# Splitting weights ahead at a fixed pace in the MLPs alone, with four chunk buffers there, and bias broadcasts issued two at a time from ScalarE's queue

## The chip, the cores and the metric

The kernel runs on one core of one Trainium2 chip. The metric is the device time of one execution in microseconds (us), taken as the median of several executions. Five engines work side by side, each through its own instructions in its own order: TensorE (PE in the rows; its weight loads are PEld), VectorE (DVE), ScalarE (ACT), GpSimd (POOL) and SyncE (SP). SP, ACT and POOL also issue the transfers (DMA), which sixteen DMA engines of the core carry.

## What is computed

The reference runs two transformer blocks, one after the other, over 512 tokens of width 1024. The first has two layers: a short-convolution mixer, an MLP, a sparse-attention mixer (NSA) and another MLP. The second block (a state-space branch and windowed attention, merged, then a gated feed-forward) follows, and the change doesn't touch it.

```
for layer in range(2):
    h = rms_norm(x, norm_mix[layer])
    if layer == 0:  x = x + short_conv_mixer(h, a_w_in, a_conv_w, a_w_out)
    else:           x = x + nsa_mixer(h, b_w_qg, b_w_o, shared, rel_bias)
    x = x + squared_relu_mlp(rms_norm(x, norm_mlp[layer]), mlp_w1[layer], mlp_w2[layer])
    if layer == 0:  shared = nsa_shared_kv(rms_norm(x, kv_norm), w_kv, ...)
squared_relu_mlp(h, w1, w2) = square(relu(h @ w1)) @ w2
```

All of it is in float32. The attention adds a bias per head and distance, which comes from a small table (`rel_bias`).

## The kernel before

**Products.** Each product of two float32 matrices is made from three TensorE matmuls on a rounded type (fp32r): both operands are split into a high part (the value rounded) and a low part (what the rounding left), and high by high, high by low and low by high are added up in PSUM. For activations the parts are called `hh`/`hl`, `a`/`b` or `yh`/`yl`, for weights `whi`/`wlo`. A matmul here takes a 128x128 weight block against 512 token columns.

**The weight stream.** All weights lie in device memory as 362 chunks of 128x1024 (512 KB), in the order in which they are used; a chunk holds eight weight blocks, and four blocks are a half. `Stream.pre` loads a chunk into one of two buffers (`w32`, on SP's queue), and splits halves up to three ahead of the one in use: ScalarE makes `whi` (L200, L207), VectorE makes `wlo` (L209), each in four buffers. `take` hands out the next block, and calls `pre` at each half. Layer A (the mixer) uses chunks 0 to 31, the first MLP (MLP0) 32 to 95, NSA 96 to 132, the second MLP (MLP1) 133 to 196.

**Splits ahead.** `Stream.ahead` (called once a chunk by `take`) makes the low parts of 112 later chunks, those of NSA and of the second block's mixer (`NSA_CH`, `MIX_CH`), beforehand: GpSimd's queue loads the chunk (`aw`, L161), ScalarE makes its high part (`ah`, L168 or L172), VectorE its low part (`al`, L169 or L173), and GpSimd's queue writes that back to device memory (`dlo`, L174). Later `pre` loads it instead of computing it. The tiles `aw` and `al` have two buffers, `ah` one. Some chunks are also scaled by a vector on the way, in four pieces (L168, L169) instead of one. Splits ahead are made in layer A, from the time when ten chunks have been asked for, in MLP0 and in MLP1, three for every four chunks.

**Biases.** In layer A, after the second output block (`f == 1`), `biases` multiplies the table with one-hot rows (six small matmuls) into `line` in device memory, and spreads each of its 16 rows over 128 rows of the arrays `sk1`, `sk2` and `sk3`, each row one element further: 48 transfers from device memory to device memory, 16 each of 320, 192 and 72 KB, issued on GpSimd's queue (L622). Attention later reads skewed rows from them.

**The order of the work.** The program is recorded as written, and a scheduler that simulates it then sets the order of the instructions on each engine. The order is fixed when the program is built, and each engine carries out its own in that order, waiting on semaphores. So a split ahead stands where that simulation put it, which may be far ahead of the place where `ahead` was called, and an engine that waits at one holds up all that stands behind it. A transfer signals on one of eight semaphores of its kind (`DMAHW0` to `DMAHW7` for SP and ACT, `DMASW0` to `DMASW7` for POOL), taken in turn; a later transfer on the same one waits until the earlier has landed.

Of the kernel before, what the change touches and what calls it, by code (L numbers as in the profile page):

```python
# [47 lines left out]
MIX_CH = (197, 272)  # L48
AHEAD0 = 10

# [75 lines left out]
class Stream:  # L126
    def __init__(self, b, pool, src, nch):
# [11 lines left out]
        self.owed = 0  # L139

    def scaled(self, half):
        g, ks = self.plan[half]
        n = 512 // len(ks)
        for i, k in enumerate(ks):
            yield slice(i * n, i * n + n), self.b.pv(g, k)

    def ahead(self):
        if self.ap is None or not self.todo or self.nd < AHEAD0:
            return
        self.owed += 3  # L150
        if self.owed < 4:
            return
        self.owed -= 4
        nc = self.b.nc
        c = self.todo.pop(0)
# [6 lines left out]
        if 2 * c in self.plan or 2 * c + 1 in self.plan:  # L162
            for o in range(2):
                e = slice(o * 512, o * 512 + 512)
                ws, hs, ls = w[:, e], h[:, e], l[:, e]
                parts = self.scaled(2 * c + o) if 2 * c + o in self.plan else [(slice(0, 512), 1.0)]
                for a, sc in parts:
                    nc.scalar.activation(out=hs[:, a], in_=ws[:, a], func=AF.Copy, scale=sc)  # L168
                    nc.vector.scalar_tensor_tensor(out=ls[:, a], in0=ws[:, a], scalar=sc, in1=hs[:, a].bitcast(F32),  # L169
                                                   op0=ALU.mult, op1=ALU.subtract)  # L170
        else:
            nc.scalar.activation(out=h, in_=w, func=AF.Copy)  # L172
            nc.vector.tensor_tensor(out=l, in0=w, in1=h.bitcast(F32), op=ALU.subtract)  # L173
# [10 lines left out]
    def pre(self, half):  # L184
        b, nc = self.b, self.b.nc
        while self.nd < min(self.nch, half // 2 + 2):
            t = self.pool.tile([P, 1024], F32, tag="w32", name="w32", bufs=2)
            nc.sync.dma_start(t, self.src[self.nd])
            self.w32[self.nd] = t
            self.nd += 1  # L190
# [41 lines left out]
class Builder:  # L232
# [230 lines left out]
    def first(self):  # L463
# [15 lines left out]
        with ExitStack() as c:  # L479
            ps = c.enter_context(tc.tile_pool(name="psA", bufs=1, space=PSUM))  # L480
            self.ps1 = lambda: ps.tile([P, 512], F32, tag="mm", bufs=7, name="mm")
            self.pst = lambda: ps.tile([P, 512], F32, tag="st", bufs=1, name="st")
            self.st.ap = c.enter_context(tc.tile_pool(name="ahead", bufs=1))
            with ExitStack() as c2:
                self.yp = c2.enter_context(tc.tile_pool(name="la", bufs=1))
                self.layer_a()
            if self.stop == "a":
                return
            self.mlp("mlp_w1_0", "mlp_w2_0", "g_mlp0")
            self.st.ap = None  # L490
# [16 lines left out]
    def layer_a(self):  # L507
# [14 lines left out]
        for f in range(KD):  # L522
            pcs = []
            for part in (1, 2, 0):
                if f == 0 and part:
                    p = (p1, p2)[part - 1]
                else:
                    p = self.ps1()
                    self.gemm([(p, XS)], "a_w_in", 0, part * 1024 + f * 128, hs)
                pcs.append(p)  # L530
                if f == 0 and part == 0:
# [25 lines left out]
        for m in range(KD):  # L557
            p = self.ps1()
            self.gemm([(p, slice(0, 512))], "a_w_out", 0, m * 128, ys)
            x = self.xs[m]  # L560
            nc.vector.tensor_tensor(out=x[:, XS], in0=p, in1=x[:, XS], op=ALU.add)
# [38 lines left out]
    def biases(self):  # L600
# [18 lines left out]
        self.sk3 = self.dr.tile([16, 128 * 145], F32, name="sk3")  # L619
        for h in range(16):  # L620
            for sk, a, n in ((self.sk1, 0, 640), (self.sk2, OH_A, 384), (self.sk3, OH_A + 384, 144)):
                nc.gpsimd.dma_start(sk[h:h + 1, :].rearrange("o (q w) -> (o q) w", w=n + 1)[:, 0:n],  # L622
                                    self.line[h:h + 1, a:a + n].to_broadcast([128, n]))

# [1256 lines left out]
```

## Time and profile before

| | us |
|---|---|
| Median of 3 runs | 2486.36 |
| Lowest and highest of them | 2483.63, 2491.55 |
| Profiled execution: its own time | 2476.05 |
| Profiled execution: span, first to last instruction | 2474.3 |
| Busy in that span: PE, PEld, DVE, ACT, POOL | 97%, 84%, 66%, 50%, 19% |

The profiled execution is one more run, 10 us below the median of the others, and 1.75 us of its time lie outside the span. Matmuls overlap, so a busy share near 100% doesn't say that TensorE goes at its best pace: how many matmuls it starts in a stretch says that.

### The profile page before, as it was taken

How to read it: one execution, taken by the hardware profiler on the slowest of the kernel's cores; microseconds unless marked ns; L12 is line 12 of the kernel's file. 1: busy time of each engine (PE TensorE's matmuls, PEld its weight loads, DVE VectorE, ACT ScalarE, POOL GpSimd, SP SyncE). 2: the span in 40 equal slices, each digit the busy share in tenths (PEclk: the TensorE clock that was granted, in tenths of full speed). 3: DMA queues.
4: the chain of work that ended last, by engine and by line, in shares of the span. 5: the costliest groups of instructions: out<-in, count | busy, mean ns of one | idle time of the engine just before them, and what ended most of it. 6: DMA issues, size and time to landing. Idle time of an engine off the chain costs nothing.

```text
span 2474.3 us, 38734 instructions
## 1 busy us (share of the span) xinstructions
PE 2391.7 (97%) x14273; PEld 2078.8 (84%) x14273; DVE 1624.5 (66%) x3293; ACT 1231.0 (50%) x2431; POOL 471.5 (19%) x657
## 2 busy tenths in 40 slices
PE   7999999999899999999999999999999999999997
PEld 5777777887787777777888999999999999998996
DVE  8657855543777768746636895569776566864873
ACT  6436543333677765434344776556555334432442
POOL 2333221001333322221022222122322100000001
PEclk9999999999999999999999999999999999999998
DMA  7898886335743347887335354543335452333322
GB/s 277 271 266 289 303 306 223 95 117 166 242 129 93 120 144 255 297 283 278 103 94 195 114 149 148 166 152 121 125 125 162 141 196 86 95 94 94 92 88 77
DMA packets 151739, 418.93 MB, mean 169 GB/s; under 512 B 22603, under 2 KB 29003, under 8 KB 151499
## 3 DMA queue, kind: packets, MB, share of 16 engines
q1 hardware_dynamic: 115024, 287.70, 36.3%
q0 software_dynamic: 35392, 127.49, 15.4%
q8 instruction: 112, 1.84, 0.3%
q10 hardware_dynamic: 1132, 1.26, 0.2%
q14 instruction: 79, 0.65, 0.1%
HBM read 340.62 MB, written 83.23 MB: 171 GB/s over the span
## 4 chain that ended last, share of the span: by engine, by line
PE 67%; issue 17%; POOL 5%; DMA 4%; DVE 4%; ACT 2%; POOLq 0%; DVEq 0%; SPq 0%; ACTq 0%
PE mm L305 53%; PE g L305 4%; PE o L305 3%; PE s L305 2%; DMA sk<-line 2%; POOL aw L161 2%; POOL dlo L174 2%; PE u L305 1%; DMA aw<-in_ws_dram 1%; PE pt L309 1%; PE u L309 1%; DVE e L728 1%; DMA w<-in_ws_dram 1%; ACT ph L313 0%; POOL acc L339 0%
## 5 line engine op out<-in xcount | busy, mean ns | idle before, releaser
L305 PE MATMUL mm<-hh,whi 128*128 128x258 f32 (+2 forms) x2464 | 799.0, 325 | 23.2 <-ACT hh L353 11.6
L305 PE MATMUL mm<-hh,wlo 128*128 128x258 f32 (+2 forms) x2464 | 798.7, 324 | 4.5 <-DVE wlo L209 4.5
L305 PE MATMUL mm<-hl,whi 128*128 128x258 f32 (+2 forms) x2464 | 798.8, 324 | 4.3 <-DVE hl L354 4.3
L207 ACT ACTIVATE whi<-w 128x512 fp32r<-128x512 f32 x500 | 308.5, 626 | 499.1 <-PE mm L305 322.7
L305 PEld LDWEIGHTS mm<-hh,whi 128*128 128x128 f32 x2464 | 464.5, 189 | 70.5 <-ACT hh L353 15.4
L209 DVE TENSOR_TENSOR wlo<-w,whi 128x512 fp32r<-128x512 f32 x498 | 347.9, 702 | 242.7 <-ACT whi L207 235.3
L305 PEld LDWEIGHTS mm<-hh,wlo 128*128 128x128 f32 x2464 | 465.3, 189 | 48.8 <-DVE wlo L209 7.4
L305 PEld LDWEIGHTS mm<-hl,whi 128*128 128x128 f32 x2464 | 465.1, 189 | 46.8 <-DVE hl L354 6.1
L305 PE MATMUL mm<-a,whi 128*128 128x512 f32 (+1 forms) x699 | 275.5, 395 | 5.1 <-ACT whi L207 4.7
L305 PE MATMUL mm<-a,wlo 128*128 128x512 f32 (+1 forms) x699 | 276.2, 395 | 3.8 <-DVE wlo L209 3.5
L305 PE MATMUL mm<-b,whi 128*128 128x512 f32 (+1 forms) x699 | 275.3, 394 | 1.8 <-DVE b L314 1.8
L173 DVE TENSOR_TENSOR al<-aw,ah 128x1024 fp32r<-128x1024 f32 x91 | 111.4, 1224 | 125.8 <-ACT ah L172 125.6
L172 ACT ACTIVATE ah<-aw 128x1024 fp32r<-128x1024 f32 x91 | 96.3, 1059 | 176.9 <-DMA aw<-in_ws_dram 169.2
L305 PEld LDWEIGHTS mm<-a,wlo 128*128 128x128 f32 x699 | 132.6, 190 | 38.5 <-DVE wlo L209 8.8
L305 PEld LDWEIGHTS mm<-a,whi 128*128 128x128 f32 x699 | 132.5, 189 | 37.4 <-ACT whi L207 6.9
L200 ACT ACTIVATE whi<-w 128x512 fp32r<-128x512 f32 x182 | 114.0, 630 | 97.1 <-PE mm L305 88.4
L305 PEld LDWEIGHTS mm<-b,whi 128*128 128x128 f32 x699 | 132.6, 190 | 32.2 <-DVE b L314 2.4
L174 POOL DMA_DIRECT2D dlo<-al x112 | 60.5, 540 | 440.1 <-DVE al L173 324.0
L305 PE MATMUL mm<-oh,whi 128*128 128x258 f32 (+1 forms) x400 | 123.8, 311 | 2.3 <-ACT oh L313 2.1
L305 PE MATMUL mm<-ol,whi 128*128 128x258 f32 (+1 forms) x400 | 124.2, 310 | 0.3 <-DVE ol L314 0.3
L305 PE MATMUL mm<-oh,wlo 128*128 128x258 f32 (+1 forms) x400 | 123.4, 308 | 0.0
L305 PEld LDWEIGHTS mm<-oh,whi 128*128 128x128 f32 x400 | 76.8, 193 | 7.7 <-ACT oh L313 2.4
(541 smaller groups left out, 4292.3 us busy)
## 6 DMA issues: line engine op xcount, KB each, us to landing
w<-in_ws_dram SPq DMA_DIRECT2D x361, 512.0 KB, 4.1
aw<-in_ws_dram POOLq DMA_DIRECT2D x112, 512.0 KB, 6.3
dlo<-al POOLq DMA_DIRECT2D x112, 512.0 KB, 4.3
wlo<-dlo SPq DMA_DIRECT2D x224, 256.0 KB, 2.9
sk<-line POOLq DMA_DIRECT2D x16, 320.0 KB, 9.4
bias<-sk SPq DMA_DIRECT2D x16, 256.0 KB, 3.2
sk<-line POOLq DMA_DIRECT2D x16, 192.0 KB, 9.7
x<-xs SPq DMA_DIRECT2D x8, 264.0 KB, 2.8
```

What stands on the lines that cost most here:

```text
L161: nc.gpsimd.dma_start(w, self.src[c])
L172: nc.scalar.activation(out=h, in_=w, func=AF.Copy)
L173: nc.vector.tensor_tensor(out=l, in0=w, in1=h.bitcast(F32), op=ALU.subtract)
L174: nc.gpsimd.dma_start(self.dlo[c], l.bitcast(F32))
L200: nc.scalar.activation(out=h[:, a], in_=src[:, a], func=AF.Copy, scale=sc)
L207: nc.scalar.activation(out=h, in_=src, func=AF.Copy)
L209: eng.tensor_tensor(out=l, in0=src, in1=h.bitcast(F32), op=ALU.subtract)
L305: self.nc.tensor.matmul(out, l, r, start=start, stop=stop)
L309: self.nc.tensor.transpose(out, in_, self.ident[0:n, 0:n])
L728: (nc.gpsimd if g in EPOOL else nc.vector).tensor_tensor(out=ev[64 * q:64 * q + 64, :, g, 0:nn], in0=src[:, q, 4 * jh:4 * jh + 4, b:b + nn ...
```

## The change

1. `ahead` works in the MLPs alone: its pool is opened after layer A, and the condition on ten chunks goes. Its rate is seven splits for eight chunks instead of three for four, so that the 112 splits fall on 128 chunks.
2. The high part of a split ahead is kept in program order on ScalarE (`keep_in_program_order`): the scheduler may no longer move it.
3. In the MLPs a chunk whose number leaves 0 or 1 over when divided by 4 is loaded into one of two further buffers (`ax`), and chunks are asked for up to four ahead instead of two.
4. The 48 bias broadcasts leave GpSimd's queue. They are issued on ScalarE's queue, two after each output block of layer A from the third on, also kept in program order, first all of `sk1`, then `sk2`, then `sk3`.

```diff
--- before.py
+++ after.py
@@ -46,7 +46,8 @@
 PPB = 9
 NSA_CH = (96, 133)
 MIX_CH = (197, 272)
-AHEAD0 = 10
+MLP_CH = ((34, 96), (135, 197))
+AHEAD = (7, 8)
 
 
 def _bucket(d):
@@ -138,6 +139,9 @@
         self.done = set()
         self.owed = 0
 
+    def aux(self, c):
+        return self.ap is not None and any(a <= c < b for a, b in MLP_CH)
+
     def scaled(self, half):
         g, ks = self.plan[half]
         n = 512 // len(ks)
@@ -145,13 +149,13 @@
             yield slice(i * n, i * n + n), self.b.pv(g, k)
 
     def ahead(self):
-        if self.ap is None or not self.todo or self.nd < AHEAD0:
+        if self.ap is None or not self.todo:
             return
-        self.owed += 3
-        if self.owed < 4:
+        self.owed += AHEAD[0]
+        if self.owed < AHEAD[1]:
             return
-        self.owed -= 4
-        nc = self.b.nc
+        self.owed -= AHEAD[1]
+        nc, pin = self.b.nc, self.b.tc.keep_in_program_order
         c = self.todo.pop(0)
         if self.dlo is None:
             self.dlo = self.b.dr.tile([self.nch, P, 1024], F32, name="dlo")
@@ -165,11 +169,11 @@
                 ws, hs, ls = w[:, e], h[:, e], l[:, e]
                 parts = self.scaled(2 * c + o) if 2 * c + o in self.plan else [(slice(0, 512), 1.0)]
                 for a, sc in parts:
-                    nc.scalar.activation(out=hs[:, a], in_=ws[:, a], func=AF.Copy, scale=sc)
+                    pin(nc.scalar.activation(out=hs[:, a], in_=ws[:, a], func=AF.Copy, scale=sc))
                     nc.vector.scalar_tensor_tensor(out=ls[:, a], in0=ws[:, a], scalar=sc, in1=hs[:, a].bitcast(F32),
                                                    op0=ALU.mult, op1=ALU.subtract)
         else:
-            nc.scalar.activation(out=h, in_=w, func=AF.Copy)
+            pin(nc.scalar.activation(out=h, in_=w, func=AF.Copy))
             nc.vector.tensor_tensor(out=l, in0=w, in1=h.bitcast(F32), op=ALU.subtract)
         nc.gpsimd.dma_start(self.dlo[c], l.bitcast(F32))
         self.done.add(c)
@@ -183,8 +187,11 @@
 
     def pre(self, half):
         b, nc = self.b, self.b.nc
-        while self.nd < min(self.nch, half // 2 + 2):
-            t = self.pool.tile([P, 1024], F32, tag="w32", name="w32", bufs=2)
+        while self.nd < min(self.nch, half // 2 + (4 if self.aux(half // 2 + 3) else 2)):
+            if self.aux(self.nd) and self.nd % 4 < 2:
+                t = self.ap.tile([P, 1024], F32, tag="ax", name="ax", bufs=2)
+            else:
+                t = self.pool.tile([P, 1024], F32, tag="w32", name="w32", bufs=2)
             nc.sync.dma_start(t, self.src[self.nd])
             self.w32[self.nd] = t
             self.nd += 1
@@ -480,12 +487,12 @@
             ps = c.enter_context(tc.tile_pool(name="psA", bufs=1, space=PSUM))
             self.ps1 = lambda: ps.tile([P, 512], F32, tag="mm", bufs=7, name="mm")
             self.pst = lambda: ps.tile([P, 512], F32, tag="st", bufs=1, name="st")
-            self.st.ap = c.enter_context(tc.tile_pool(name="ahead", bufs=1))
             with ExitStack() as c2:
                 self.yp = c2.enter_context(tc.tile_pool(name="la", bufs=1))
                 self.layer_a()
             if self.stop == "a":
                 return
+            self.st.ap = c.enter_context(tc.tile_pool(name="ahead", bufs=1))
             self.mlp("mlp_w1_0", "mlp_w2_0", "g_mlp0")
             self.st.ap = None
         if self.stop == "mlp0":
@@ -527,6 +534,7 @@
                 else:
                     p = self.ps1()
                     self.gemm([(p, XS)], "a_w_in", 0, part * 1024 + f * 128, hs)
+                    self.skew_out()
                 pcs.append(p)
                 if f == 0 and part == 0:
                     d = self.stat1(acc, 1024, self.pst, (0, 0))
@@ -557,6 +565,7 @@
         for m in range(KD):
             p = self.ps1()
             self.gemm([(p, slice(0, 512))], "a_w_out", 0, m * 128, ys)
+            self.skew_out()
             x = self.xs[m]
             nc.vector.tensor_tensor(out=x[:, XS], in0=p, in1=x[:, XS], op=ALU.add)
 
@@ -617,10 +626,17 @@
         self.sk1 = self.dr.tile([16, 128 * 641], F32, name="sk1")
         self.sk2 = self.dr.tile([16, 128 * 385], F32, name="sk2")
         self.sk3 = self.dr.tile([16, 128 * 145], F32, name="sk3")
-        for h in range(16):
-            for sk, a, n in ((self.sk1, 0, 640), (self.sk2, OH_A, 384), (self.sk3, OH_A + 384, 144)):
-                nc.gpsimd.dma_start(sk[h:h + 1, :].rearrange("o (q w) -> (o q) w", w=n + 1)[:, 0:n],
-                                    self.line[h:h + 1, a:a + n].to_broadcast([128, n]))
+        self.skews = [(h, sk, a, n) for sk, a, n in ((self.sk1, 0, 640), (self.sk2, OH_A, 384), (self.sk3, OH_A + 384, 144))
+                      for h in range(16)]
+
+    skews = ()
+
+    def skew_out(self):
+        for _ in range(min(2, len(self.skews))):
+            h, sk, a, n = self.skews.pop(0)
+            self.tc.keep_in_program_order(
+                self.nc.scalar.dma_start(sk[h:h + 1, :].rearrange("o (q w) -> (o q) w", w=n + 1)[:, 0:n],
+                                         self.line[h:h + 1, a:a + n].to_broadcast([128, n])))
 
     def skew(self, sk, h, n):
         return sk[h:h + 1, 0:128 * n].rearrange("o (q w) -> (o q) w", w=n)
```

Three places show how this moves instructions. The first is the start of the program on ScalarE, before: `hh` and `sq` belong to the input tiles `x`, and `ah` is a split ahead.

```order
L207 ACTIVATE whi_181<-w32_81 128x512
L168 ACTIVATE ah_693<-aw_692,pkt_74 128x128 x8
L353 ACTIVATE hh_119<-x_66,pkt_74 128x512
L334 ACTIVATE sq_151<-x_66 128x512
L168 ACTIVATE ah_749<-aw_748,pkt_74 128x256 x4
L353 ACTIVATE hh_123<-x_67,pkt_74 128x512
L334 ACTIVATE sq_153<-x_67 128x512
L207 ACTIVATE whi_185<-w32_81 128x512
```

The same place on ScalarE now:

```order
L214 ACTIVATE whi_178<-w32_81 128x512
L360 ACTIVATE hh_116<-x_66,pkt_74 128x512
L341 ACTIVATE sq_148<-x_66 128x512
L360 ACTIVATE hh_120<-x_67,pkt_74 128x512
L341 ACTIVATE sq_150<-x_67 128x512
L214 ACTIVATE whi_182<-w32_81 128x512
L360 ACTIVATE hh_124<-x_68,pkt_74 128x512
L341 ACTIVATE sq_154<-x_68 128x512
```

The two splits ahead that stood between the first weights and the first input tiles are gone. On VectorE their low parts stood at the same place, and are gone too.

The second place is ScalarE in layer A, where the first broadcasts are issued now (with the semaphores that each row waits for; `yh` is a high part of the mixer's output):

```order
L214 ACTIVATE whi_769<-w32_767 128x512 [waits DMAHW4_49,PE_49,Activation_49]
L638 DMA sk1_493<-line_490 128x640 [waits DMAHW6_49]
L638 DMA sk1_493<-line_490 128x640 x5
L638 DMA sk1_493<-line_490 128x640 [waits DMAHW5_49]
L638 DMA sk1_493<-line_490 128x640
L638 DMA sk1_493<-line_490 128x640 [waits DMAHW7_49]
L638 DMA sk1_493<-line_490 128x640 [waits DMAHW0_49]
L638 DMA sk1_493<-line_490 128x640 [waits DMAHW1_49]
L638 DMA sk1_493<-line_490 128x640 [waits DMAHW2_49]
L320 ACTIVATE yh_762<-o_760 128x512 [waits DVE_49]
L214 ACTIVATE whi_785<-w32_767 128x512 [waits PE_49,Activation_49]
L638 DMA sk1_493<-line_490 128x640 [waits DMAHW3_49]
```

Twelve broadcasts stand in a row there, since `line` isn't written earlier, and then two after every other weight half. Before, all 48 stood on POOL, one behind the other; its first rows were these.

```order
L161 DMA aw_1730<-in_ws_dram 128x1024 [waits DMASW5_49,Activation_49]
L622 DMA sk1_496<-line_493 128x640 [waits DMAHW6_49,DMASW2_49]
L622 DMA sk2_497<-line_493 128x384
L622 DMA sk3_498<-line_493 128x144 [waits DMASW4_49]
L622 DMA sk1_496<-line_493 128x640
L622 DMA sk2_497<-line_493 128x384 [waits DMASW6_49]
```

The third place is ScalarE in MLP1, in the product with `w2`, before:

```order
L207 ACTIVATE whi_10041<-w32_10016 128x512
L207 ACTIVATE whi_10059<-w32_10057 128x512
L172 ACTIVATE ah_10547<-aw_10546 128x1024
L207 ACTIVATE whi_10082<-w32_10057 128x512
L207 ACTIVATE whi_10102<-w32_10100 128x512
L172 ACTIVATE ah_10633<-aw_10632 128x1024
L207 ACTIVATE whi_10118<-w32_10100 128x512
L172 ACTIVATE ah_10683<-aw_10682 128x1024
L207 ACTIVATE whi_10136<-w32_10134 128x512
L207 ACTIVATE whi_10159<-w32_10134 128x512
L172 ACTIVATE ah_10733<-aw_10732 128x1024
```

The same product now:

```order
L214 ACTIVATE whi_10252<-w32_10173 128x512
L176 ACTIVATE ah_10257<-aw_10256 128x1024
L214 ACTIVATE whi_10275<-w32_10173 128x512
L214 ACTIVATE whi_10295<-ax_10216 128x512
L176 ACTIVATE ah_10300<-aw_10299 128x1024
L214 ACTIVATE whi_10318<-ax_10216 128x512
L214 ACTIVATE whi_10336<-ax_10250 128x512
L176 ACTIVATE ah_10341<-aw_10340 128x1024
L214 ACTIVATE whi_10359<-ax_10250 128x512
```

There is one split ahead for exactly two weight halves (one chunk) now, and none in every eighth chunk. Before, the scheduler had set one for 1.57 halves on the average of MLP1 (46 splits in 72 halves, with none in the last 50 halves), and in MLP0 and layer A much the same until all were made.

## Rows read from the trace of the kernel before

**Rows 1.** Windows by stage: length, each engine's busy time (instructions), PEclk, DMA share, GB/s

```profile
222.00:410.00 188.00, 179.81 (x757) 140.65 (x757) 124.42 (x193) 84.77 (x124) 39.21 (x74) 1.00 0.86 299
425.00:575.00 150.00, 150.00 (x649) 121.69 (x648) 75.00 (x109) 50.22 (x81) 6.55 (x5) 1.00 0.34 106
1044.00:1180.00 136.00, 128.17 (x525) 100.79 (x524) 74.66 (x97) 53.37 (x76) 25.43 (x48) 0.96 0.78 276
```

**Rows 2.** Windows again: the start, and the stretch of the broadcasts

```profile
0.00:39.73 39.73, 21.65 (x67) 15.09 (x68) 29.74 (x77) 24.20 (x50) 13.50 (x19) 0.91 0.77 271
101.00:161.00 60.00, 55.41 (x232) 44.00 (x232) 29.45 (x47) 16.14 (x30) 26.20 (x50) 0.97 0.99 242
```

**Rows 3.** ACT's timeline at the start: start us, us, instruction, [idle before, releaser]

```profile
3.54 0.63 ACT L207 ACTIVATE whi<-w 128x512 fp32r<-128x512 f32 x1 [0.74 <-DMA w<-in_ws_dram]
7.93 2.44 ACT L168 ACTIVATE ah<-aw,pkt 128x128 fp32r<-128x128 f32 x8 [3.76 <-DMA aw<-in_ws_dram]
10.28 0.70 ACT L353 ACTIVATE hh<-x,pkt 128x512 fp32r<-128x512 f32 x1
10.90 0.61 ACT L334 ACTIVATE sq<-x 128x512 f32<-128x512 f32 x1
11.42 1.69 ACT L168 ACTIVATE ah<-aw,pkt 128x256 fp32r<-128x256 f32 x4
```

**Rows 4.** DVE's timeline in the same stretch

```profile
11.02 0.75 DVE L354 SCALAR_TENSOR_TENSOR hl<-x,pkt,hh 128x512 fp32r<-128x512 f32 x1 [0.26 <-ACT hh L353]
...
16.88 1.76 DVE L354 SCALAR_TENSOR_TENSOR hl<-x,pkt,hh 128x512 fp32r<-128x512 f32 x1
```

**Rows 5.** POOL's timeline: sums of squares at the start, and the first broadcasts

```profile
16.47 6.67 POOL L339 TENSOR_TENSOR acc<-acc,sq 128x512 f32<-128x512 f32 x4
...
101.57 4.19 POOL L622 DMA_DIRECT2D sk<-line  x8 [2.95 <-DMA line<-la]
106.85 0.52 POOL L622 DMA_DIRECT2D sk<-line  x1 [1.09 <-DMA sk<-line]
```

**Rows 6.** Waits from 101 to 161 us: POOL's longest (total us, times, longest)

```profile
POOL sk L622 <- DMA sk<-line: 29.0, 27, 2.7
```

**Rows 7.** Transfers from 100 to 162 us: times issued, size, median us to landing

```profile
sk<-line POOLq DMA_DIRECT2D x16, 320.0 KB, 9.4
w<-in_ws_dram SPq DMA_DIRECT2D x10, 512.0 KB, 9.6
```

**Rows 8.** ACT's timeline: a transfer that ACT issues itself

```profile
1.26 0.57 ACTq L605 DMA_DIRECT2D oh<-in_oh_dram  x1
```

**Rows 9.** PE's waits, 100 to 175 us

```profile
PE mm L305 <- ACT whi L207: 4.9, 3, 2.7
```

**Rows 10.** PE's waits in MLP0, 222 to 587 us

```profile
PE mm L305 <- DVE wlo L209: 3.9, 6, 1.2
PE st L305 <- DVE dh L408: 2.0, 1, 2.0
```

**Rows 11.** PE's waits in MLP1, 939 to 1316 us

```profile
PE mm L305 <- ACT whi L207: 5.5, 4, 2.4
```

**Rows 12.** ACT's waits in MLP1, 1044 to 1180 us

```profile
ACT ah L172 <- DMA aw<-in_ws_dram: 61.9, 24, 5.1
ACT whi L207 <- DMA w<-in_ws_dram: 10.3, 4, 3.5
```

**Rows 13.** Windows inside that stretch: one hundred microseconds of MLP1

```profile
1050.00:1150.00 100.00, 93.86 (x379) 73.58 (x378) 49.46 (x62) 37.90 (x53) 20.36 (x39) 0.95 0.80 285
```

**Rows 14.** Transfers of MLP1, 1044 to 1180 us

```profile
w<-in_ws_dram SPq DMA_DIRECT2D x23, 512.0 KB, 5.8
aw<-in_ws_dram POOLq DMA_DIRECT2D x23, 512.0 KB, 6.9
```

**Rows 15.** The page's costliest groups: the two steps of a split ahead

```profile
L173 DVE TENSOR_TENSOR al<-aw,ah 128x1024 fp32r<-128x1024 f32 x91 | 111.4, 1224 | 125.8 <-ACT ah L172 125.6
L172 ACT ACTIVATE ah<-aw 128x1024 fp32r<-128x1024 f32 x91 | 96.3, 1059 | 176.9 <-DMA aw<-in_ws_dram 169.2
```

## The prediction

> **What bounds the kernel now.** I read the busy shares first, then windows by stage, and then, where TensorE starts fewer matmuls than it could, its waits and the timelines of the engines that feed it. The shares say that TensorE has work 97% of the time, so the question is its pace. In a stretch of MLP0 with no splits ahead it starts 649 matmuls of 512 columns in 150 us, one every 0.231 us, without idle time [rows 1]. That is the pace to hold the other stages of 512-column matmuls against. Three of them fall short.
>
> *The start.* 67 matmuls have started by 39.73 us [rows 2]; at 0.231 they are 15.5 us of work. ScalarE has the first weights split at about 4.1 us, then waits until 7.93 for a chunk to be split ahead, works 2.3 us on it, makes the first `hh` at 10.28, and then does a second split ahead of 1.6 us [rows 3]. VectorE does the low parts at the same places.
>
> *The broadcasts.* From 101 to 161 us TensorE starts 232 matmuls, worth 53.6 us: 6.4 us are lost, of which 4.9 are waits for `whi` [rows 2, 9], as the weight chunks take 9.6 us to land there [rows 7], with the DMA engines 0.99 busy.
>
> *The MLPs while splits ahead run.* MLP0 from 222 to 410 us: 757 matmuls, 174.9 us of work in 188, so 13.1 lost. MLP1 from 1044 to 1180: 525, 121.3 in 136, so 14.7 lost [rows 1]. The waits before TensorE name `whi` and `wlo` [rows 10, 11], and behind them ScalarE stands 61.9 us of the 136 at splits ahead that wait for `aw`, against 10.3 for a chunk of its own [rows 12]. The clock is 0.96 in that stretch of MLP1 as against 1.00 in the quiet one: a stall also costs slow matmuls after it; the counts hold that too.
>
> Why ScalarE waits there can be worked out. GpSimd issues 39 transfers in 100 us of MLP1, two to a split, so a split ahead takes 5.1 us [rows 13]. The loop of one buffer gives the same: 6.9 us for `aw` to land [rows 14], 1.06 and 1.22 us for the two halves of the split [rows 15], and two issues at 0.5 us [rows 5] are 10.2 us, with two buffers 5.1. The order on ScalarE puts a split ahead after every 1.57 halves, and a half is 12 matmuls, 2.77 us: 4.35 us of TensorE's work. The order asks for a split each 4.35 us, the loop gives one each 5.1, and as the weights of the current product stand behind it in ScalarE's order, TensorE falls back to the pace of the loop.
>
> **The change, part by part**, against the profiled execution's own 2476.05 us, which is 10.3 below the median shown.
>
> *No splits ahead at the start.* ScalarE's way to the eighth `hh` is then eight `hh` of 0.62 us, seven `sq` and three `whi` of 0.52 (starts in [rows 3]): 10.2 us from 4.2, so 14.4, if the inputs have landed. VectorE is later: its steps take 1.76 us instead of 0.75 while GpSimd sums squares [rows 4, 5], and these sums stay. Five sums at 1.6 us cover about 6.6 to 15 us, in which five of the nine steps still due fit; the other four and an addition at 0.75 end at about 18.5. From there 20 matmuls remain to the 67th: it starts at about 23.5, a gain of 16. Bounds: with only the two splits' ScalarE time gone (2.3 + 1.6) 4 us; with TensorE unhindered from 4.2 us, 39.7 - 19.7 = 20. I take 16, as nothing that held the rest (two more splits ahead, the load of two chunks in front of the inputs) is left. Layer A has no other loss that splits cause, beside the broadcasts.
>
> *Pace and buffers in the MLPs.* A split ahead now stands at every 2 halves, 5.54 us of TensorE's work, above the 5.1 us that the loop takes, and each eighth chunk has none, which gives back 5.5 us. So the loop no longer holds ScalarE. The transfers in seven chunks of eight are as many as now per unit of work, three of 512 KB in 5.54 us or 284 GB/s, no more than the 285 that flow now at a share of 0.80 [rows 13]; a chunk lands in 5.8 us [rows 14], and with four buffers it is asked for some 16 us ahead. That takes away what the splits cost in MLP0, 13.1 less 2.0 of a wait for the norm's `dh` [rows 10] and 1 for its extra matmuls: 10; and in MLP1 14.7. The stretches that were quiet (MLP0's last 177 us, MLP1's last 136) get splits now. Their price is the work of ScalarE and VectorE, 1.06 and 1.22 us [rows 15] in 5.54, where each has half its time free [rows 1]: covered, and 2 to 3 us each stage if it isn't. At the start of each MLP the first `aw` loads wait for the pool, and at its end one split stands before the next stage's first steps: 1.22 us each [rows 15]; I put 1.5 in all.
>
> *Broadcasts from ScalarE.* Same bytes, same DMA engines, already 0.99 busy [rows 2], so the transfers end no earlier at best than TensorE's own stalls allow. New is what stands behind them: twelve in a row on ScalarE, ahead of `whi` of the 28th half, and the last four wait for the first four to land. The issues cost about 0.5 us each [rows 8], 6 us for twelve. The first broadcast now lands 5.3 us after its issue [rows 5], and the 48 fill about 60 us [rows 2, 6], 3.7 for each three of 584 KB, so 2.0 for one of 320 KB. The fourth lands 10 to 11 us after `line`. By the order of its matmuls TensorE has 2.5 halves, 6.9 us, of weights left when `line` lands. So a stall of 3 to 5, a second of about 2 (the next chunk's load on SP waits for the eighth broadcast, its semaphore), and slow matmuls behind: 8 us instead of 6.4, a loss of 1.6. Bounds: 0 if the pace of two for 5.54 us lets all of it hide, a gain of 6.4; and 25 if most of the later pairs hold ScalarE too (29 of the 48 issues have a wait), a loss of 18.6. I take 8, as the pairs after the twelfth ask for 640 KB in 5.54 us, 4 us of such transfers, and catch up.
>
> The Trainium skill, page "DMA: Bandwidth & Descriptors", section "Issuing engines are not separate DMA queues", says that transfers of all issuing engines run on the same 16 DMA engines and interleave, and that another issuing engine saves only the time of issuing. By that rule this part is worth nothing, and the stage keeps its 6.4 us; the sum would be 1.6 lower than mine. The share of 0.99 agrees with it; the rule doesn't speak of what waits behind the issues on ScalarE, which my 8 us prices.
>
> *Sum:* 2476.05 - 16 - 10 - 14.7 + 1.5 + 1.6 = 2438.5, that is 37.6 less; taken off the median of 2486.4 it is 2449.
>
> **The rivals.**
> *(a) The MLPs keep their loss.* 284 GB/s in the runs of seven is today's rate of transfers; if `aw` still lands late, ScalarE, which may no longer move a split, waits as now. For it: 61.9 us of waits at that rate [rows 12]. Against: these come from an order that asks every 4.35 us, and the eighth chunk resets the lag. Then 24.7 us come back: 2474.
> *(b) ScalarE is held by the broadcasts* up to the bound above, 25 us instead of 8: 2466.
> *(c) Slower.* GpSimd waited at 27 of its 48 issues, 29.0 us [rows 6], with nothing urgent behind; on ScalarE all weights stand behind. If a broadcast from this queue lands as late as now (9.4 us [rows 7]) and the splits get through only between them, the 60 us that the 48 take become a stall of TensorE instead of 6.4: 53.6 more, against 39.2 gained elsewhere: 14 over the median, 2501. It decides from 46 us of stall, 1.6 us for each of the 29 waiting issues. Against it: TensorE's halves in hand absorb 7 us each time, and two in three broadcasts are the smaller ones.
> *(d) Everything hides:* the broadcasts too, and the wait for `dh` in MLP0: 1.6 + 6.4 + 2.0 more, 2439.
>
> **How the numbers follow.** Forecast 0.66, 2449 (its own range 2441 to 2461); (a) 0.11, (b) 0.12, (c) 0.05, (d) 0.06. From 2437 to 2470 lie the forecast, (d) and (b): 0.84. Below or above 0.3%, 7.5 us, a measurement of this kernel can tell from no change: faster takes the forecast, (b), (d) and most of (a), 0.92; (c) gives slower 0.05; 0.03 lies between.
>
> **What would show it.** Right: the 67th matmul starts near 24 us; no `ah` before MLP0; in both MLPs 108 or so matmuls in each 25 us from end to end, and ScalarE's waits for `aw` down to a tenth; 56 splits in each MLP, spread evenly to its end. In layer A, one stall of 3 to 5 us after `line` lands, on `whi`, and a smaller one about 10 us later. Wrong: `hh` still late at the start because inputs land late; ScalarE at splits waiting for `aw` with TensorE idle behind; or a row of stalls on `whi` through all of layer A, one to each pair of broadcasts.

## The result, and the profile after

The changed kernel takes 2446.98 us (median of 4 runs, 2442.72 to 2447.67), the kernel before beside it 2488.34 (4 runs, 2483.63 to 2491.55): a ratio of 0.9843, 95% interval 0.982 to 0.9866. The prediction was 2449. Its profiled execution took 2447.41 us; its span is 28.7 us shorter than that of before.

To see where the time went, count TensorE's matmuls in the order in which they start (14273 in each trace) and take the time between the same two:

| matmuls | work there | before, us | after, us | predicted, us | measured, us |
|---|---|---|---|---|---|
| to the 67th | start | 39.7 | 29.1 | -16 | -10.6 |
| 67 to 200 | layer A | 31.8 | 31.9 | 0 | 0 |
| 200 to 700 | layer A, broadcasts | 125.1 | 134.9 | +1.6 | +9.8 |
| 700 to 2350 | end of layer A, MLP0 | 396.4 | 384.1 | -10 | -12.4 |
| 2350 to 4300 | attention between the MLPs | 390.6 | 390.5 | +1.5 (here and behind MLP1) | -0.1 |
| 4300 to 5300 | MLP1 | 247.8 | 231.6 | -14.7 | -16.1 |
| 5300 to the end | the rest | 1242.8 | 1243.5 | | +0.7 |

The windows of the changed kernel over MLP0's two halves and over the same stretch of work in MLP1, with the columns of [rows 1]:

```profile
206.00:392.00 186.00, 186.00 (x802) 150.47 (x801) 128.99 (x251) 94.47 (x181) 32.26 (x59) 1.00 0.75 259
392.00:574.00 182.00, 181.24 (x783) 146.66 (x781) 121.11 (x159) 88.78 (x136) 35.29 (x59) 1.00 0.78 264
1030.00:1166.00 136.00, 136.00 (x589) 110.31 (x588) 81.91 (x108) 57.04 (x81) 22.64 (x43) 1.00 0.75 260
```

802 matmuls in 186 us are one every 0.232 us, and the 589 in 136 us of MLP1 were 525 before [rows 1]. GpSimd issues in both halves of MLP0 now (59 instructions each), so the splits reach its end. ScalarE's waits in MLP1, 1044 to 1180 us, hold no `aw` any more, as against 61.9 us [rows 12]; it waits for TensorE to free a buffer, which is slack:

```profile
ACT whi L214 <- PE mm L312: 60.3, 39, 2.2
ACT a L320 <- DVE q L596: 16.8, 11, 1.6
```

Layer A is where it went the other way. TensorE's two long stalls there in the timeline, the counterpart of [rows 9] (all of 4.9 us):

```profile
101.73 0.79 PE L312 MATMUL mm<-hh,whi 128*128 128x512 f32 x1 [6.26 <-ACT whi L214]
118.29 0.79 PE L312 MATMUL mm<-hh,whi 128*128 128x512 f32 x1 [5.57 <-ACT whi L214]
```

and ScalarE's and its queue's timeline behind them (start, duration, instruction, and what ended the idle time before it):

```profile
86.28 14.21 ACTq L638 DMA_DIRECT2D sk<-line  x12
100.53 0.63 ACT L320 ACTIVATE yh<-o 128x512 fp32r<-128x512 f32 x1 [15.67 <-DMA sk<-line]
...
101.07 0.61 ACT L214 ACTIVATE whi<-w 128x512 fp32r<-128x512 f32 x1
...
117.61 0.63 ACT L214 ACTIVATE whi<-w 128x512 fp32r<-128x512 f32 x1 [8.60 <-DMA w<-in_ws_dram]
```

The twelve issues hold ScalarE for 14.2 us, and `whi` of the next half comes behind them. Taken one by one they are not alike. The fourth lasts 0.62 us, the fifth 1.20, the ninth 1.70 and the twelfth 1.47:

```profile
88.15 0.62 ACTq L638 DMA_DIRECT2D sk<-line  x1
88.80 1.20 ACTq L638 DMA_DIRECT2D sk<-line  x1
94.33 1.70 ACTq L638 DMA_DIRECT2D sk<-line  x1
99.01 1.47 ACTq L638 DMA_DIRECT2D sk<-line  x1
```

The last four wait for the semaphores of the first four, but those had landed: the first broadcast lands 4.7 us after its issue, at 91.0 us, and the fourth 9.8 us after its own, at 98.0.

```profile
sk<-line ACTq DMA_DIRECT2D x1, 320.0 KB, 4.7
sk<-line ACTq DMA_DIRECT2D x1, 320.0 KB, 9.8
```

So it isn't a wait for a landing that stretches the fifth to the twelfth issue; they themselves last 1.0 to 1.7 us, with four and more broadcasts under way. Why they do isn't shown.

The chunk for the second stall was late because SP's queue stood too, in its waits from 84 to 135 us:

```profile
SPq L195 <- DMA sk<-line: 25.7, 2, 23.3
```

Its load takes the semaphore of the eighth broadcast, which was issued at 93.29 us and landed 12.9 us later; the load goes out at 106.28.

The matmuls after the stalls were slow as well. The windows of layer A:

```profile
90.00:100.00 10.00, 5.47 (x24) 4.12 (x22) 0.69 (x1) 0.00 (x0) 0.00 (x0) 1.00 0.90 184
100.00:110.00 10.00, 8.27 (x25) 6.45 (x26) 4.20 (x7) 3.02 (x5) 0.00 (x0) 0.66 0.96 225
110.00:120.00 10.00, 4.43 (x16) 3.26 (x15) 2.30 (x4) 1.57 (x3) 0.00 (x0) 0.86 0.69 200
120.00:130.00 10.00, 10.00 (x36) 7.94 (x36) 4.59 (x9) 3.15 (x6) 0.00 (x0) 0.80 0.71 187
```

After 6.3 us without a matmul the granted clock averages 0.66 in the next 10 us, so most of that time lies at the lower of the two levels (1.2 of 2.4 GHz). In the last of these windows TensorE is busy throughout and starts 36 matmuls where 43 fit.

### The profile page after: what moved, and what is told of

Its sections match the earlier page's. It is cut to its first block, busy times and chain, and to the rows that moved or that the text cites. A ratio compares the mean times of both kernels' runs of the same rounds, so it can differ in the third digit from the quotient of the medians.

```text
span 2445.6 us, 38763 instructions
## 1 busy us (share of the span) xinstructions
PE 2381.8 (97%) x14273; PEld 2082.8 (85%) x14273; DVE 1637.1 (67%) x3293; ACT 1235.3 (51%) x2431; POOL 446.4 (18%) x609
## 4 chain that ended last, share of the span: by engine, by line
PE 91%; DVE 4%; DMA 2%; ACT 2%; issue 1%; ACTq 0%; SPq 0%; DVEq 0%
PE mm L312 76%; PE g L312 4%; PE o L312 3%; PE s L312 3%; PE u L316 1%; PE u L312 1%; PE pt L316 1%; DMA w<-in_ws_dram 1%; DVE e L744 1%; DMA sk<-line 1%; ACT ph L320 0%; PE st L312 0%; DVE pl L321 0%; PE o L316 0%; DVE xs L1610 0%
## 5 line engine op out<-in xcount | busy, mean ns | idle before, releaser
L312 PE MATMUL mm<-hh,whi 128*128 128x258 f32 (+2 forms) x2464 | 797.7, 325 | 23.5 <-ACT whi L214 12.5
L312 PEld LDWEIGHTS mm<-hh,whi 128*128 128x128 f32 x2464 | 464.6, 189 | 67.6 <-ACT whi L214 14.2
L312 PEld LDWEIGHTS mm<-hl,whi 128*128 128x128 f32 x2464 | 465.3, 189 | 45.6 <-issue 4.3
L214 ACT ACTIVATE whi<-w 128x512 fp32r<-128x512 f32 x378 | 237.2, 631 | 483.4 <-PE mm L312 364.5
L216 DVE TENSOR_TENSOR wlo<-w,whi 128x512 fp32r<-128x512 f32 x376 | 264.0, 704 | 219.9 <-ACT whi L214 210.8
L207 ACT ACTIVATE whi<-w 128x512 fp32r<-128x512 f32 x182 | 114.1, 630 | 96.9 <-PE mm L312 86.1
L214 ACT ACTIVATE whi<-ax 128x512 fp32r<-128x512 f32 x122 | 76.8, 631 | 146.7 <-PE mm L312 146.6
L216 DVE TENSOR_TENSOR wlo<-ax,whi 128x512 fp32r<-128x512 f32 x122 | 83.8, 689 | 70.2 <-ACT whi L214 70.0
```

The source lines that it names most:

```text
L207: nc.scalar.activation(out=h[:, a], in_=src[:, a], func=AF.Copy, scale=sc)
L214: nc.scalar.activation(out=h, in_=src, func=AF.Copy)
L216: eng.tensor_tensor(out=l, in0=src, in1=h.bitcast(F32), op=ALU.subtract)
L312: self.nc.tensor.matmul(out, l, r, start=start, stop=stop)
```

## The experiments

Medians are of the runs of each kernel; the kernel before ran beside each group (2491.15, 2489.89 and 2489.0 us), and ratios are against it. The stretches by matmul count are those of the table above; in us, from one profile each:

| kernel | to 67th | 200-700 | 700-2350 | 4300-5300 |
|---|---|---|---|---|
| before | 39.7 | 125.1 | 396.4 | 247.8 |
| changed | 29.1 | 134.9 | 384.1 | 231.6 |
| e1_no_pin | 28.2 | 135.1 | 404.4 | 258.7 |
| e2_two_buffers | 29.3 | 135.3 | 384.1 | 231.6 |
| e3_skews_late | 27.8 | 117.5 | 385.9 | 231.6 |
| e4_skews_pool | 27.7 | 125.5 | 384.1 | 231.6 |
| e5_pin_only | 31.0 | 128.0 | 385.6 | 231.6 |
| e6_before_again | 40.0 | 130.1 | 399.4 | 248.8 |
| e7_late_burst | 28.3 | 131.4 | 384.1 | 231.6 |
| e8_late_sums | 24.4 | 117.5 | 385.2 | 231.6 |
| e9_aw_four | 29.4 | 135.7 | 384.1 | 231.6 |
| e10_late_sums_fours | 25.5 | 117.5 | 384.0 | 231.6 |

One profile has a spread of its own. The start is the same in seven kernels (changed, e1 to e4, e7, e9), and takes 27.7 to 29.4 us in them; in the two profiles of the kernel before (the first row and e6), 200 to 700 takes 125.1 and 130.1.

**e1, the splits not held to their place** (changed kernel):

```diff
-        nc, pin = self.b.nc, self.b.tc.keep_in_program_order
+        nc, pin = self.b.nc, lambda i: i
```

> The changed kernel, with ScalarE's half of each split ahead no longer held to its place in the program; rate of seven in eight, four chunk buffers and broadcasts stay. On ScalarE a split ahead then stands at every 1.6 halves again instead of every 2. Theory (pace): that asks for one each 4.4 us where the loop of a split's buffers gives one each 5.1, so ScalarE waits at splits for aw, TensorE at whi and wlo in both MLPs, and 20 to 28 us come back: 2467 to 2475. Rival (buffers): what cured the MLPs is that chunks are asked for four ahead; then nothing changes, 2447.

2492.63 us, ratio 1.0011 (0.9996 to 1.0027): the whole gain is gone, with rate, place and four chunk buffers kept. More came back than expected, 45.6 us of the medians: 20.3 in MLP0 and 27.0 in MLP1, where all 112 splits run now: 48 of them stand between the 4300th and the 5300th matmul, against 36 in the kernel before and in the changed one. ScalarE in MLP1, 1044 to 1180 us, and the issues there (count, KB, median us to landing):

```profile
ACT ah L176 <- DMA aw<-in_ws_dram: 73.3, 23, 5.6
```
```profile
DMA packets 10699, 39.02 MB, mean 287 GB/s; under 512 B 1187, under 2 KB 1187, under 8 KB 10692
...
aw<-in_ws_dram POOLq DMA_DIRECT2D x27, 512.0 KB, 6.6
```

27 splits in 136 us are one each 5.04 us, the 5.1 that the loop of two buffers was worked out to give.

**e2, two chunk buffers** (changed kernel):

```diff
-        while self.nd < min(self.nch, half // 2 + (4 if self.aux(half // 2 + 3) else 2)):
-            if self.aux(self.nd) and self.nd % 4 < 2:
+        while self.nd < min(self.nch, half // 2 + 2):
+            if False:
```

> The changed kernel with two chunk buffers in the MLPs as before, no ax; the pace stays. Theory (pace): a chunk lands in about 6 us and with two buffers is asked for about one chunk (5.5 us) ahead of its use by ScalarE, which itself is up to three halves ahead: at most a few us of waits for w, 2447 to 2453. Rival (buffers): both MLPs fall back to their old loss, 24 us: 2471.

2446.39 us, ratio 0.9825 (0.9794 to 0.9856), and both MLPs as in the changed kernel. With the splits held to their place, the four buffers do nothing.

**e9, four buffers for `aw`, no pin** (on e1 with the edit of e2):

```diff
-        w = self.ap.tile([P, 1024], F32, tag="aw", name="aw", bufs=2)
+        w = self.ap.tile([P, 1024], F32, tag="aw", name="aw", bufs=4)
```

> The kernel of e1_no_pin with four buffers for aw instead of two, and two chunk buffers in the MLPs instead of four (the same space). ScalarE's halves of the splits stand 1.5 halves apart in the order, a split per 4.2 us of TensorE's work. Theory (a loop of aw's two buffers gives only one split each 5.1 us): four buffers halve the loop, ScalarE waits no more, and the MLPs lose nothing: 2447 to 2455. Rival (the transfers are the limit: three of 512 KB in 4.2 us would be 374 GB/s, and 313 is what e1 moved): the splits stay 5 us apart, the MLPs keep their loss: 2480 to 2495.

2446.61 us, ratio 0.9827 (0.981 to 0.9844). The splits still stand 1.5 halves apart, and the MLPs lose nothing. Its windows row, issues and ScalarE's waits over 1044 to 1180 us:

```profile
1044.00:1180.00 136.00, 136.00 (x589) 110.31 (x588) 91.53 (x121) 65.57 (x90) 28.55 (x54) 1.00 0.88 315
```
```profile
aw<-in_ws_dram POOLq DMA_DIRECT2D x25, 512.0 KB, 7.1
```
```profile
ACT whi L214 <- PE mm L312: 30.7, 25, 2.2
ACT whi L214 <- DMA w<-in_ws_dram: 15.6, 10, 2.9
ACT ah L176 <- DVE al L177: 15.0, 14, 2.1
```

No wait for `aw` is left, though one takes longer to land (7.1 us against 6.6) and more bytes flow (315 GB/s against 287). In e9 ScalarE has done its part of MLP1's splits by 1166 us, so the pace is read from the 190 us in which they run: the steps on `ah` there (VectorE, then ScalarE), first in e9 and then in e1.

```profile
975.00:1165.00 190.00, 53.65 (x44) 46.55 (x44) 1.00 0.93 335
990.00:1180.00 190.00, 45.83 (x38) 40.28 (x38) 0.98 0.83 290
```

44 splits are one each 4.3 us, what the order asks for; 38 are one each 5.0. So the transfers were not the limit; the number of buffers was.

**e5, the pin alone** (kernel before):

```diff
-        nc = self.b.nc
+        nc, pin = self.b.nc, self.b.tc.keep_in_program_order
...
-                    nc.scalar.activation(out=hs[:, a], in_=ws[:, a], func=AF.Copy, scale=sc)
+                    pin(nc.scalar.activation(out=hs[:, a], in_=ws[:, a], func=AF.Copy, scale=sc))
...
-            nc.scalar.activation(out=h, in_=w, func=AF.Copy)
+            pin(nc.scalar.activation(out=h, in_=w, func=AF.Copy))
```

> The kernel before with one edit: ScalarE's half of each split ahead is held to its place in the program. Splits in layer A, rate of three in four, two chunk buffers and broadcasts from GpSimd all stay. In the order the first split now stands behind the 21st half instead of the first. Theory (the order of the splits is nearly the whole change): the start gains its 11 us too, and both MLPs their loss: 2476 - 11 - 25 = 2440 by the profile of before, 2440 to 2452, as some splits still stand 1.5 halves apart in layer A and the first of MLP0. Rival (the rate and the place of the splits matter as well): 2460 or more.

2443.52 us, ratio 0.9811 (0.9792 to 0.983): holding the splits to their place, three lines, is worth the whole change. Start and MLPs are within 2 us of the changed kernel's; 200 to 700, with splits beside the broadcasts, takes 128.0, between the two profiles of the kernel before.

**e4, the broadcasts back on GpSimd** (changed kernel):

```diff
-        self.skews = [(h, sk, a, n) for sk, a, n in ((self.sk1, 0, 640), (self.sk2, OH_A, 384), (self.sk3, OH_A + 384, 144))
-                      for h in range(16)]
+        for h in range(16):
+            for sk, a, n in ((self.sk1, 0, 640), (self.sk2, OH_A, 384), (self.sk3, OH_A + 384, 144)):
+                nc.gpsimd.dma_start(sk[h:h + 1, :].rearrange("o (q w) -> (o q) w", w=n + 1)[:, 0:n],
+                                    self.line[h:h + 1, a:a + n].to_broadcast([128, n]))
```

> The changed kernel with the 48 broadcasts issued by GpSimd in one go, as in the kernel before. Theory (ScalarE held): the stage loses about 6.4 us as before instead of 17: 2436, or a little less as no splits ahead run beside them. Rival (DMA engines full whoever issues): 2444 to 2449. A third: without splits ahead in layer A, GpSimd is not slowed between its issues, the broadcasts crowd together and weights land later than before: 2450 or more.

2437.11 us, ratio 0.9791 (0.9762 to 0.9819): 9.9 us under the changed kernel, and 9.4 of it lie between the 200th and the 700th matmul. So the move of the broadcasts to ScalarE cost the changed kernel that much. `w` lands later here than in the changed kernel (10.4 us against 7.1), and TensorE has one stall of 4.6 us for `whi`. Issued by GpSimd the broadcasts keep one length, and their waits for landings lie between them. Shortest, median and longest of the 48 issues in ns, here and in the changed kernel:

```profile
L631 POOL DMA_DIRECT2D sk<-line x48: 522/523/726, 84.9 to 144.1; - x48
L638 ACTq DMA_DIRECT2D sk<-line x48: 477/619/1929, 86.3 to 199.5; - x48
```

**e3, the broadcasts on ScalarE, but later** (changed kernel; `skew_out` is called in MLP0's first product too):

```diff
     def skew_out(self):
+        if self.skews and self.hold:
+            self.hold -= 1
+            return
         for _ in range(min(2, len(self.skews))):
...
+    hold = 6
```

> The changed kernel with the first two broadcasts at the seventh output block from where they may begin, not the first, so that none stands on ScalarE before line has landed and there is no row of twelve; two per block from there, the last ones in MLP0's first blocks. Theory (ScalarE held by the row of twelve): the two stalls of 6.3 and 5.6 us at whi and the slow matmuls behind them go, about 17 us lost become 2 to 7: 2432 to 2437. Rival (the 16 DMA engines are full whoever issues and when): the stalls spread out but keep their sum, 2444 to 2449.

2428.54 us, ratio 0.9757 (0.9728 to 0.9786), under the range that its theory gave. The stretch takes 117.5 us; 500 matmuls at 0.231 are 115.6. Its windows, against those of the changed kernel above:

```profile
90.00:100.00 10.00, 10.00 (x45) 8.13 (x44) 4.54 (x7) 2.62 (x4) 0.00 (x0) 1.00 0.96 217
100.00:110.00 10.00, 10.00 (x45) 8.14 (x44) 5.48 (x9) 3.16 (x5) 0.00 (x0) 1.00 0.85 193
```

and ScalarE beside its queue: an issue pair takes 1.2 us, and waits for nothing.

```profile
85.64 0.63 ACT L214 ACTIVATE whi<-w 128x512 fp32r<-128x512 f32 x1 [2.15 <-PE mm L312]
85.66 1.19 ACTq L643 DMA_DIRECT2D sk<-line  x2
```

**e7, twelve at once, later** (e3):

```diff
-        for _ in range(min(2, len(self.skews))):
+        for _ in range(min(12 if len(self.skews) == 48 else 2, len(self.skews))):
```

> The kernel of e3_skews_late (first broadcasts at the seventh output block) with twelve broadcasts there at once and two per block after, so the row of twelve stands on ScalarE when line has long landed. Theory (a wait for line holds ScalarE): only the issues cost, 12 of some 0.6 us against 7 us of weights in hand: 2428 to 2434. Rival (the row of twelve itself, four transfers of 320 KB in flight and each next issue waiting for the first to land, with the weight loads behind them): the stalls of the changed kernel return, 2440 to 2448.

2440.46 us, ratio 0.9801 (0.9781 to 0.9822): the rival's number; my theory, that a wait for `line` was the cost, fell. On the clock the row even starts at the same time, 86.2 us, in both: the changed kernel's twelve are the pairs of six blocks that piled up behind `line`, and the wait itself was at most the 1.4 us between ScalarE's `whi` (84.23, 0.63 long) and the first issue. The rival's reason, that each next issue waits for a landing, isn't borne out either: of the fifth to the twelfth only the tenth begins with a landing, 0.6 us after the ninth ended. The first four issues go out in 2.5 us, the next eight take 13.1, and ScalarE stands with them:

```profile
86.22 2.50 ACTq L643 DMA_DIRECT2D sk<-line  x4
...
88.78 13.07 ACTq L643 DMA_DIRECT2D sk<-line  x8
101.95 0.63 ACT L214 ACTIVATE whi<-w 128x512 fp32r<-128x512 f32 x1 [12.55 <-DMA sk<-line]
```

SP's queue waits again for a broadcast, which in e3 and e4 it doesn't:

```profile
SPq L195 <- DMA sk<-line: 23.6, 2, 19.9
```

**e8, the first norm's sums on VectorE** (e3):

```diff
-                (nc.vector if k >= 6 else nc.gpsimd).tensor_tensor(
+                (nc.vector if k >= 6 or late else nc.gpsimd).tensor_tensor(
```

> The kernel of e3_skews_late with all sums of squares of the first norm on VectorE (0.68 us each there) and none on GpSimd. Theory (GpSimd's sums slow VectorE's hl and wlo from 0.7 to 1.7 us): the 67th matmul starts at 23 to 25 us instead of 28 to 29.5, and the time is 3 to 5 us below that of e3: 2423 to 2426. Rival (five more additions stand between the hl on VectorE, or the inputs set the pace): 67th matmul at 27 to 30, 2427 to 2431.

2426.07 us, ratio 0.974 (0.9723 to 0.9758). The 67th matmul starts at 24.4 us, as its theory had it. VectorE at the same `hl` in the changed kernel, with GpSimd adding, and then in this one:

```profile
10.22 3.48 DVE L361 SCALAR_TENSOR_TENSOR hl<-x,pkt,hh 128x512 fp32r<-128x512 f32 x2
```
```profile
10.40 0.75 DVE L361 SCALAR_TENSOR_TENSOR hl<-x,pkt,hh 128x512 fp32r<-128x512 f32 x1
11.07 0.68 DVE L346 TENSOR_TENSOR acc<-acc,sq 128x512 f32<-128x512 f32 x1
11.67 0.74 DVE L361 SCALAR_TENSOR_TENSOR hl<-x,pkt,hh 128x512 fp32r<-128x512 f32 x1
```

An `hl` and an addition take 1.4 us there, less than one `hl` beside GpSimd. The start is 3.4 us shorter than e3's, yet the two profiles end 0.3 apart: the stretch behind the 5300th matmul, where the two kernels have the same code, took 1241.1 us in e3's and 1243.7 in this one's, and that from the 2350th to the 4300th 388.9 and 389.7. The medians are 2.5 us apart, and the intervals of e3 and e8 overlap.

**e10, the last sixteen broadcasts four to a block** (e8):

```diff
-        for _ in range(min(2, len(self.skews))):
+        for _ in range(min(4 if len(self.skews) <= 16 else 2, len(self.skews))):
```

> The kernel of e8_late_sums with the last 16 broadcasts, 72 KB each, four to an output block instead of two, so that all end within layer A. Theory (broadcasts in MLP0's first blocks cost 1.9 us there, between the 825th and the 1100th matmul): 65 us in that stretch become 63.6, 2423 to 2425. Rival (that stretch's norm waits for something else, or four in a row hold ScalarE): 2426 to 2430.

2423.74 us (2421.5 to 2424.37), ratio 0.9736 (0.9718 to 0.9754): the fastest of all, 23 us under the changed kernel, though its interval doesn't part it from e8. In its profile the stretch of MLP0 is 1.2 us shorter than e8's, as the theory had it; the start is 1.1 longer, with the same code.

**e6, the kernel before once more**, unedited.

> The kernel before, unedited, for a second profile of it. Its first profiled execution was 12 us below the median of its other runs. Theory: the difference lies where the loop of the splits ahead sets the pace, so this profile shows 51 to 54 us for 200 matmuls there (49 to 54 in the first, 46.2 without splits) and every other stage within 2 us of the first: 2484 to 2495. Rival: it is spread over all stages in proportion.

2489.96 us in this group (ratio 1.0001, 0.9983 to 1.0018); the profiled execution took 2484.71, 8.7 more than the first. Both answers fell as to the place: the MLPs take the same (MLP1 248.8 against 247.8), and 5.0 us of it lie between the 200th and 700th matmul, 3.0 behind them up to the 2350th: by the 825th matmul, in MLP0's first part, the second is 8.1 us behind. Splits ahead and broadcasts run side by side in much of that stretch; that this is the cause isn't shown.

## Why the prediction was right, point by point

The mechanism of the largest part, the MLPs, was right. The time was right within 2 us, but that is in part luck: two sizes were wrong, and they were covered by a third.

*Start, -16 predicted, -10.6 measured.* The term that was mis-sized is VectorE's way to the last `hl`. Five of the nine steps fit beside GpSimd's sums, as it had them, but all of it lay some 2 us later: the first `hh` came at 5.97 us, not 4.2, after 1.57 us of waiting for `x`, and the sums ran from 8.4 to 16.5 us, so the last `hl` ended at 20.9 us instead of 18.5. And "from there 20 matmuls remain to the 67th" was wrong: 33 did. TensorE had stood for an `hl`, and was slow behind it. Its timeline, and the windows of the 4 us after the stall and of the rest:

```profile
17.80 0.50 PE L312 MATMUL mm<-hl,whi 128*128 128x512 f32 x1 [2.38 <-DVE hl L361]
18.13 0.56 PE L312 MATMUL mm<-hh,wlo 128*128 128x512 f32 x1
18.49 0.63 PE L312 MATMUL mm<-hl,whi 128*128 128x512 f32 x1
18.92 0.63 PE L312 MATMUL mm<-hh,wlo 128*128 128x512 f32 x1
```
```profile
17.50:21.50 4.00, 3.70 (x10) 2.90 (x11) 4.00 (x12) 0.73 (x2) 0.00 (x0) 0.59 0.68 147
21.50:29.10 7.60, 7.60 (x32) 5.87 (x31) 4.59 (x19) 1.89 (x3) 0.00 (x0) 0.99 0.42 129
```

The granted clock averages 0.59 there, mostly the lower level again. That GpSimd's sums are behind the stall e8 shows: without them there is none, and the 67th matmul starts at 24.4 us, 3.4 earlier than in e3, from which it differs in nothing else. The forecast was 23.5, the changed kernel has 29.1.

*Broadcasts, +1.6 predicted, +9.8 measured.* The place and the waiting instruction were as forecast, the size was not. The term that was mis-sized is the row of issues: at "about 0.5 us each" twelve were to cost 6 us, and they held ScalarE for 14.2, as the fifth to the twelfth took 1.0 to 1.7 us each. The prediction let ScalarE go when the fourth broadcast lands, 10 to 11 us after `line`; it landed after 11.7, and none of the last four issues had to "wait for the first four to land": the issues themselves went on until 14.2 us after `line`. So the first stall was 6.3 us where "3 to 5" was taken. SP's load did wait for the eighth broadcast's semaphore, as forecast, but stood 23.3 us, and the second stall was 5.6 instead of "about 2"; slow matmuls follow each, and the later pairs did not "catch up" in time for it. The added loss lies midway between forecast and rival (b). By e6's profile of the kernel before it would be 4.8 us (134.9 against 130.1); against e4, with the issues back on GpSimd, it is 9.4. e4 and e3 show that the move to ScalarE is not bad by itself: two at a time hide, and twelve in a row cost TensorE 15.8 us over its own pace in e7, 19.3 in the changed kernel (115.6 us for the 500 matmuls). The Trainium skill's page "DMA: Bandwidth & Descriptors", section "Issuing engines are not separate DMA queues", says that another issuing engine saves only the time of issuing, and by it this part had no price. The trace doesn't agree: with the same bytes, issued by ScalarE instead of GpSimd, the stretch takes 134.9 us instead of 125.5 (e4; there the three sizes also take turns). The issuing engine decides what stands behind an issue that takes long, and the spacing how long it takes: spread out on ScalarE the same broadcasts leave 117.5 us, and 1.9 more in MLP0 (e3).

*MLPs, -24.7 predicted, -28.5 measured.* The working holds in each step: a loop of two `aw` buffers gives a split each 5.04 us (e1), the order is what asked for more (e5 and e1, from both sides), and transfers were not the limit (e9: one each 4.3 us with four buffers). What was credited wrongly is a part: the four chunk buffers have no share (e2), and the rate of seven in eight has none that can be seen, since e5 keeps three in four.

*New late splits, +1.5 predicted, +0.6 measured* from the stages behind the MLPs (-0.1 and +0.7). These profiles can't tell it from nothing: with one and the same order of splits the same two stretches differ by up to 4.6 and 3.6 us between the changed kernel and e2, e3, e4, e7, e8 and e10.

*From the profile to the median.* These parts sum to 28.7, the difference of the two spans, and the prediction took 37.6 off the median of before: 8.9 us too much. The medians differ by 41.4: the first profiled execution of before was 12.3 us under the median beside this result, that of the changed kernel only 0.4 over its own. So the kernel before runs 12.7 us further from its first profile than the changed one from its own, and the two errors nearly cancel. That is luck: the prediction saw the offset (10.3 us then) and assumed that both kernels have it. Against e6's profile the span is 37.3 us shorter. e6 places 8 of the 12 in layer A and MLP0's first part, by one profile; the other 4 to 5 were not found.

*Rivals.* (a) fell: no wait for `aw` is left. (c) would have needed stalls of 46 us; all that 200 to 700 loses is 19.3, with the slow matmuls. (d) is what e3 did by another order.

## What to carry to other kernels

When an engine waits for a prefetched tile, divide the whole loop of one buffer (landing, the steps that read it, the issues) by the number of buffers, and compare it with the interval at which the engine's order asks for it: either a sparser order or more buffers cures it, and each alone was enough here. Transfers issued from an engine that also computes should be spread out: two per 5.5 us hid here (e3), twelve in a row cost 14 us more (e7) to 17 (changed kernel), and how long each issue lasts shows it. And where two queues share semaphores, a load can wait for a transfer of the other queue. And take a gain off the median only with a second profile of the kernel before, when the first lies at the edge of its runs.

## What the runs showed of the hardware

The issue of a transfer on ScalarE's queue has no fixed length. In the changed kernel the first four of twelve broadcasts take 0.6 us each and the next eight 1.0 to 1.7, with no landing to wait for; in e3, two at a time, a pair takes 1.2. On GpSimd's queue (e4) the median issue takes 0.52 us and the longest 0.73, and the first eight go out in 4.4 us.

A broadcast from DRAM to DRAM held the DMA engines longer for each byte than a weight load. In the changed kernel from 84 to 135 us, by queue (packets, MB, share of 16 engines):

```profile
q10 hardware_dynamic: 3260, 6.56, 61.6%
q1 hardware_dynamic: 868, 3.18, 17.2%
```

That is 9.4% of the window for each MB of `sk` (q10) and 5.4% for each MB of `w` (q1), 1.7 times as much. The rows of `sk` are also shorter, 640 or 384 numbers against 1024, so this doesn't tell which of the two it is.

What looks like one queue standing behind another is the program's own: SP's and ScalarE's transfers take the same eight semaphores in turn, and so SP's `w` waited 23.3 us for an `sk` that ScalarE had issued, and 19.9 in e7; in e3, without a row of twelve on ScalarE, and in e4, where the broadcasts have GpSimd's semaphores, no load did.
